# A streaming-encoder layer on one core: the second latent up projection and the chunk heads' output projection taken in turn, and latent units that wait for half of an up projection

## The chip, the core and the metric

The kernel runs on one core of a Trainium2 chip. The metric is the device time of one execution in microseconds (us). Five engines take part, each with its own queue of instructions that it works through in order: TensorE (PE, matrix multiply; its weight loads are shown as PEld), VectorE (DVE), ScalarE (ACT), GpSimd (POOL) and SyncE (SP), which here issues all DMA transfers. Matrix products land in PSUM banks and are moved to SBUF by ACT or DVE.

## The reference, cut to what matters

The sequence has 1024 rows of 1024 columns. One layer is computed:

```python
h = modulate(rmsnorm(x, g_attn_norm), sh_a, sc_a)
proj = h @ w_in                           # split into q_lat 256, kv_lat 128, k_rope 32, ca_qkv 1536
q  = rmsnorm(q_lat) @ w_q_up              # latent up projections: 8 heads x 96
kv = rmsnorm(kv_lat) @ w_kv_up            # 8 heads x (64 + 64)
o_mla = mla_attention(rope(rmsnorm(q)), rope(rmsnorm(k)), v)   # causal by chunks of 64, 8 latent heads
o_ca  = chunk_attention(cq, ck, cv, rel_bias)                  # band of 9 chunks, 8 chunk heads
x = x + g_a * (concat([o_mla, o_ca]) @ w_out)
h = modulate(rmsnorm(x, g_mlp_norm), sh_m, sc_m)
u = causal_dwconv(h @ w_up)               # 2 x 2816 columns
x = x + g_m * ((silu(gate) * val) @ w_down)
```

The rows of `w_out` fall in two halves: 0 to 511 multiply the latent heads' output, 512 to 1023 the chunk heads' output. So half of the output projection can be done as soon as all chunk heads are done.

## The kernel before, in words

Products in full precision are made of three matmuls of a high and a low part (`gemm3`, L207; `gemm3_f`, L219, the same cut into steps). The layer runs in three parts: the entry and the attention (to about 644 us of the span), the output projection of the latent heads with the second norm (to about 700 us), and the channel MLP with the two big projections. The change touches the attention part alone.

**Units.** The attention is cut into 32 units (list `specs`, L1184): 16 chunk units (0 to 15) and 16 latent units (16 to 31). A unit is one head and one half `g` of its query rows; units alternate `g` = 0 (4 key blocks) and `g` = 1 (8 key blocks). A unit has a preparation (`prep`: transposes of q and k, the tiles `mq_ps` and `mk_ps` for latent units, and their copies into `qt` and `kt`), four `guard` steps (a score pass for the row minimum), `mrow`, then per key block `st` (scores `tc` or `tm`, exponential into `p`, a high and a low half `hl`) and `val` (the product with the values, `pv`). The high half is made by ACT or, for every second block, by POOL (L1053, L1055). While unit n runs its blocks, unit n+2 is prepared and unit n+1 is guarded.

**Fillers.** Projections are generators that are advanced between the blocks (`fillers`, L1131): the chunk heads' input projections `v0`, `qk1` to `qk3`, `v1`, the latent projection `m` (L709), the two latent up projections `up0` and `up1` (`f_up`, L833; `up0` feeds latent units 16 to 23, `up1` units 24 to 31), and `oca` (L885), the chunk heads' half of the output projection. `pace` (L1178) compares the attention cost so far with a polyline `knots` (L1174) and advances the first filler in the list until its cost is on the line; up-projection steps count 3.2 times their cost (`UP_W`). `need` (L1164) advances the fillers without regard to pace until a named one has ended; a latent unit's preparation calls it with `up0` or `up1`.

**An up projection** works on 8 row tiles t. Per tile: a product `qu` (6 matmuls of 384 columns), a product `ku` (3 matmuls of 512 columns), copies by ACT (`uqr` L794, `kraw` L807, `vm` L601), squares (L796, L811), sums by DVE; and per pair of tiles an inverse root, scalings (DVE L823, ACT L828) and the rotary part on POOL (L829, L704 to L707). The scaled rows are `qn` and `kn`, which the preparations transpose.

**The chunk heads' output projection** `oca` makes 16 products (2 column halves n, 8 row tiles t), each of 12 matmuls of 512 columns (two steps of 6). Its weights come through `wo_steps` (L844): per part of 256 columns a load `wor`, a gating by POOL (L860, times the gate row in `gabc`), a high part by ACT (L81) and a low part by POOL (L87). The first set of weights is advanced once per step in the second half of `up1` (L837 to L839), and what is left of it is taken all at once when `oca` begins (L903). Each product's left side is loaded from DRAM (`cl`) and split into `ch` and `cl`, in tiles of the pool "R" that the projections use too.

The instructions are written in this order, but a scheduler then sets the final order on each engine: attention instructions have a higher priority (`OFF_S`, `OFF_V`), and filler instructions are held behind named earlier ones (`tied`, `trail`).

Of the kernel before, what the change touches and what calls it, by code (L numbers as in the profile page):

```python
# [46 lines left out]
SIDE = 1150  # L47
HI_ON, HL_BUFS = "pa", 3
VSCALE = 2.0 ** 14
O_EARLY = 0.2  # L50
UP_W = 3.2


C_C, C_GA, C_GM, C_B, C_GQL, C_GKL = 0, 8, 16, 24, 72, 74
# [14 lines left out]
def layer_kernel(ctx, tc, I, out):  # L69
# [517 lines left out]
            qk_norm(pt[:], f"{p}_{t}", qns[p, t // 4], t % 4)  # L587

    def v_tiles(pl, name, n):
        vs = [pl.tile([P, 4, 2, 3, 64], F16, name=f"{name}{i}") for i in range(n)]  # L590
# [164 lines left out]
    def f_up_steps(gr):  # L755
# [27 lines left out]
        for t in range(NT):  # L783
            h, j = divmod(t, 4)
            sl = slice(j * P, (j + 1) * P)
            if t % 2 == 0:
                mq[gr, t // 2] = g3([P, 2, 4, QK], F32, f"qn{gr}_{t}")
                mk[gr, t // 2] = g3([P, 2, 4, QK], F32, f"kn{gr}_{t}")
                mv[gr, t // 2] = G["vs"][4 * gr + t // 2]
# [41 lines left out]


    def f_up(gr):  # L833
        steps_in[0] = 0
        for c in f_up_steps(gr):
            yield c * UP_W
            steps_in[0] += gr  # L837
            if steps_in[0] > 8 * gr and gr:
                next(wo_next[0], None)  # L839

    gab = []
    wos = {}

    def wo_steps(k0, n):  # L844
        parts = [(k, c) for k in range(k0, k0 + 4) for c in range(2)]
        raws = []
        ws = wos[k0, n] = []

        def load(i):
            if i < len(parts):  # L850
                k, c = parts[i]
                raws.append(atile(f"wor{k}_{n}_{c}"))
                c0 = n * 512 + c * 256
                sp.dma_start(raws[i][:], I["w_out"][k * P:(k + 1) * P, c0:c0 + 256])

        def gated(i):
            if i < len(parts):
                c0 = n * 512 + parts[i][1] * 256
                with tied("p"):
                    pool.tensor_tensor(raws[i][:], raws[i][:], gab[0][:, c0:c0 + 256], op=MUL)  # L860

        load(0)
        load(1)
        yield
        gated(0)
        yield
        for i, (k, c) in enumerate(parts):
            load(i + 2)
            gated(i + 1)
            if c == 0:  # L870
                ws.append(g4([P, 2, 512], F32R, f"wo{k}_{n}"))
            cc = slice(c * 256, c * 256 + 256)
            tied_hi_lo(ws[-1][:, 0, cc], ws[-1][:, 1, cc], raws[i][:])
            yield

    def first_wo():
        while not ga_done:
            next(side[0])
        gab.append(pgtile([P, D], F32, "gabc"))
        sp.dma_start(gab[0][:], ga_d[:])  # L880
        yield from wo_steps(4, 0)

    wo_next = [first_wo()]

    def f_oca():  # L885
        cl, ch, xo = {}, {}, {}
        todo = [(n, t) for n in range(2) for t in range(NT)]

        def load(i):
            if i < len(todo):  # L890
                n, t = todo[i]
                cl[i] = rtile(f"cl{t}_{n}", (P, 4, P), F32R)
                sp.dma_start(f32(cl[i][:]), oT_d[4:8, :, t * P:(t + 1) * P].rearrange("k p t -> p k t"))

        def conv(i):
            if i < len(todo):
                n, t = todo[i]
                ch[i] = rtile(f"ch{t}_{n}", (P, 4, P), F32R)
                tied_hi_lo(ch[i][:], cl[i][:], f32(cl[i][:]))

        load(0)
        load(1)
        for _ in wo_next[0]:  # L903
            pass
        conv(0)
        yield 0
        for i, (n, t) in enumerate(todo):
            if t == 0:
                for _ in wo_next[0]:
                    pass  # L910
                ws = wos[4, n]
                wo_next[0] = wo_steps(0, 0) if n else wo_steps(4, 1)
            o = qtile(f"co{t}_{n}")
            sp.dma_start(o[:], I["x"][t * P:(t + 1) * P, n * 512:(n + 1) * 512])
            load(i + 2)
            conv(i + 1)
            pt = ps.tile([P, 512], F32, name=f"oc{t}_{n}", tag="mm", bufs=2)
            hi, lo = ch.pop(i), cl.pop(i)
            for c in gemm3_f(pt[:], [(hi[:, k], lo[:, k], ws[k][:, 0], ws[k][:, 1]) for k in range(4)]):
                yield c  # L920
                next(wo_next[0], None)
            with tied("v"):
                dve.tensor_tensor(o[:], o[:], pt[:], op=ADD)
            sp.dma_start(part_d[t][:, n * 512:(n + 1) * 512], o[:])


    NK, NQ = 4, 3
    kts = [at.tile([P, 2, 512], F16, name=f"kt{i}") for i in range(NK)]
# [180 lines left out]
    def mla_unit(n, gr, hh, g):  # L1109
        u = Unit(n, f"m{gr}{hh}", g, False, hh % 2,  # L1110
                 lambda b: (mv[gr, b // 2], 2 * (b % 2) + hh // 2),
                 oT_d[2 * gr + hh // 2][64 * (hh % 2):64 * (hh % 2) + 64], ("m", gr))

        def prep():
            with tc.high_priority(offset=OFF_S):
                pt = turned(lambda j: mq[gr, (4 * g + j) // 2][:, j % 2, hh, :], QK, f"mq{gr}{hh}_{g}")
                sq = scm[:QK, 2:3]
                act.activation(u.q[:QK, 0], pt[:QK], AF.Copy, scale=sq)
                dve.scalar_tensor_tensor(u.q[:QK, 1], pt[:QK], sq, u.q[:QK, 0], op0=MUL, op1=SUB)
                pt = turned(lambda j: mk[gr, (4 * g + j) // 2][:, j % 2, hh, :], QK, f"mk{gr}{hh}_{g}")  # L1120
# [12 lines left out]
    spent = [0.0]  # L1133
    done = set()
    side = [f_ada()]
# [5 lines left out]
    def fill_step():  # L1141
        while fillers:
            key, gen = fillers[0]
            if key == "oca" and not ca_done or key == "v1" and not p0_done:
                return None
            try:
                c = next(gen)
# [1 line left out]
                done.add(key)  # L1149
                fillers.pop(0)  # L1150
                continue
            spent[0] += c
            if key not in ("v0", "up0", "up1", "oca"):
                nside[0] += c
                while nside[0] > SIDE:
                    nside[0] -= SIDE
# [7 lines left out]
    def need(keys):  # L1164
        for k in keys:
            while k not in done:
# [486 lines left out]
```

## Time and profile before

| | |
|---|---|
| median of 3 runs | 1395.44 us (1393.77 to 1395.97) |
| the profiled execution | 1393.72 us, its span 1391.5 us |
| mean granted TensorE clock | 0.962 |
| chunk units' scores `tc` | from 87 to 406 us of the span |
| up projections' products `qu`, `ku` | from 357 to 474 us |
| latent units' scores `tm` | from 419 to 641 us |
| chunk heads' output products `oc` | from 491 to 639 us |
| latent heads' output products `op` | from 651 to 700 us |

A table of stretches has one row for each stretch of the span: its length, then for PE, PEld, DVE, ACT and POOL the busy time and in brackets the number of instructions, then the granted clock of TensorE (1.00 is full speed), the share of DMA time and GB/s. A row of the timeline has the start, the duration, engine, line, operation, output <- input, and in square brackets how long the engine sat idle before and what it waited for. A row of a tile's view has the shortest, median and longest duration in ns and the first and last start.

### The profile page before, as it was taken

To read this page: it belongs to the slowest core of one execution; us is meant where nothing else is said; L and a number is where in the kernel's file an instruction comes from. 1 tells how busy PE (TensorE), PEld (TensorE's weight loads), DVE (VectorE), ACT (ScalarE), POOL (GpSimd) and SP (SyncE) were. 2 spreads that over 40 slices of the span, in tenths; PEclk is the share of its full clock that TensorE was granted. 3 is DMA by queue.
4 is the path that set the end of the run, shared out by engine and by line. 5 is a ranking of instruction groups with operands and counts; after the bars stand their busy time and mean duration, and the time that the engine had idled before them with its cause. 6 is when DMAs were issued, how large, how long until landed. Compare 5 with 4: busy or idle time off the path is not lost.

```text
span 1391.5 us, 20573 instructions
## 1 busy us (share of the span) xinstructions
PE 1295.8 (93%) x7140; PEld 884.3 (64%) x7140; DVE 1029.7 (74%) x1512; ACT 817.3 (59%) x1584; POOL 745.1 (54%) x844
## 2 busy tenths in 40 slices
PE   8888999999878899997989989999999979999998
PEld 7877788878545466555844434444444438888887
DVE  7758887776668867674679989888888875566564
ACT  5646676566778767664786566666666533333331
POOL 5844434244453572443533876666666626666563
PEclk7999999999979899998999999999999989999999
DMA  9412333222000243225516422222211006446443
GB/s 352 135 39 79 100 100 96 79 77 62 24 23 20 59 142 96 87 95 183 214 46 234 144 98 92 91 91 92 82 71 61 31 31 219 151 144 244 163 145 106
DMA packets 85764, 153.06 MB, mean 110 GB/s; under 512 B 8854, under 2 KB 49050, under 8 KB 85660
## 3 DMA queue, kind: packets, MB, share of 16 engines
q1 hardware_dynamic: 85660, 151.75, 32.6%
q8 instruction: 56, 0.92, 0.3%
q14 instruction: 48, 0.39, 0.1%
HBM read 122.88 MB, written 28.84 MB: 109 GB/s over the span
## 4 chain that ended last, share of the span: by engine, by line
PE 68%; DVE 12%; ACT 6%; POOL 5%; issue 5%; DMA 4%; SPq 0%; POOLq 0%; ACTq 0%; DVEq 0%
PE p L1326 8%; PE p L1325 8%; PE p L1327 8%; PE dn L1567 6%; PE dn L1568 6%; PE dn L1569 6%; PE tm L1045 3%; PE tc L1045 1%; DMA aw<-w_ada 1%; PE op L211 1%; DMA x<-x 1%; PE op L213 1%; PE op L212 1%; PE oc L211 1%; PE pvm L1072 1%
## 5 line engine op out<-in xcount | busy, mean ns | idle before, releaser
L87 POOL TENSOR_TENSOR wds<-wd,wds 128x512 fp32r<-128x512 f32 x88 | 152.4, 1752 | 104.2 <-ACT wds L81 104.1
L1567 PE MATMUL dn<-wds,g 128*128 128x512 f32 x352 | 136.8, 395 | 9.1 <-ACT g L81 9.1
L81 ACT ACTIVATE wds<-wd 128x512 fp32r<-128x512 f32 x88 | 54.7, 624 | 152.4 <-PE dn L1569 152.4
L1568 PE MATMUL dn<-wds,g 128*128 128x512 f32 x352 | 136.7, 391 | 0.0
L1554 DVE TENSOR_TENSOR wd<-wd,gmbc 128x1024 f32<-128x1024 f32 x44 | 73.8, 1680 | 84.1 <-DMA wd<-w_down 84.1
L1569 PE MATMUL dn<-wds,g 128*128 128x512 f32 x352 | 135.3, 389 | 0.0
L1056 DVE TENSOR_TENSOR hlm<-pm,hlm 128x512 f16<-128x512 f32 (+1 forms) x96 | 64.6, 682 | 35.7 <-POOL hlm L83 22.4
L1406 ACT ACTIVATE u<-c,pk,wcv 128x1024 f32<-128x1024 f32 x44 | 52.2, 1232 | 51.1 <-DVE c L1446 43.9
L1567 PEld LDWEIGHTS dn<-wds,g 128*128 128x128 f32 x352 | 67.1, 191 | 23.7 <-ACT g L81 9.6
L87 DVE TENSOR_TENSOR g<-gr,g 128x512 fp32r<-128x512 f32 x44 | 71.0, 1614 | 6.7 <-ACT g L81 6.4
L1568 PEld LDWEIGHTS dn<-wds,g 128*128 128x128 f32 x352 | 66.6, 189 | 13.7
L1045 PE MATMUL tm<-qt,kt 96*128 96x512 f16 (+7 forms) x288 | 69.6, 338 | 6.0 <-ACT hlm L1053 2.4
L1569 PEld LDWEIGHTS dn<-wds,g 128*128 128x128 f32 x352 | 66.1, 188 | 13.8
L83 POOL TENSOR_SCALAR hlm<-pm 128x384 f16<-128x384 f32 (+2 forms) x48 | 25.2, 525 | 92.4 <-PE pvm L1074 44.7
L1407 DVE SCALAR_TENSOR_TENSOR u<-c,wcv,u 128x1023 f32<-128x1023 f32 x44 | 56.0, 1308 | 24.4 <-ACT u L1406 24.4
L1049 ACT ACTIVATE pm<-tm,scm 128x512 f32<-128x512 f32 (+1 forms) x96 | 55.2, 580 | 31.4 <-PE tm L1045 24.0
L1056 DVE TENSOR_TENSOR hlc<-pc,hlc 128x256 f16<-128x256 f32 (+3 forms) x96 | 52.1, 547 | 22.5 <-POOL hlc L83 11.7
L1045 PEld LDWEIGHTS <-kt 128*128 128x128 f16 (+2 forms) x480 | 45.7, 100 | 34.9 <-issue 16.9
L1049 ACT ACTIVATE pc<-tc,sca 128x512 f32<-128x512 f32 (+3 forms) x96 | 50.3, 525 | 29.9 <-DVE hlc L1056 13.4
L1002 DVE TENSOR_REDUCE mz<-sm 128x1 f16<-128x128 f32 (+3 forms) x64 | 48.2, 753 | 20.4 <-PE sm L1000 17.3
L81 ACT ACTIVATE wd<-wu 128x512 f16<-128x512 f32 x22 | 13.9, 630 | 83.6 <-DVE wu L1337 83.6
L1318 POOL TENSOR_TENSOR wa<-wu,wa 128x512 f16<-128x512 f32 x22 | 35.4, 1609 | 50.3 <-ACT wa L81 50.1
(470 smaller groups left out, 4551.0 us busy)
## 6 DMA issues: line engine op xcount, KB each, us to landing
wu<-w_up SPq DMA_DIRECT2D x44, 512.0 KB, 4.0
wd<-w_down SPq DMA_DIRECT2D x44, 512.0 KB, 3.6
aw<-w_ada SPq DMA_DIRECT2D x96, 128.0 KB, 2.2
g_d<-u SPq DMA_DIRECT2D x22, 512.0 KB, 2.6
gr<-g_d SPq DMA_DIRECT2D x44, 256.0 KB, 3.0
adaw<-w_ada_a SPq DMA_DIRECT2D x16, 512.0 KB, 6.8
x<-x SPq DMA_DIRECT2D x8, 512.0 KB, 7.5
wq_r<-w_qk SPq DMA_DIRECT2D x32, 128.0 KB, 2.4
```

Of the source, the lines that this page charges most:

```text
L81: return act.activation(o, i, AF.Copy)
L87: return (pool if eng == "p" else dve).tensor_tensor(o, i, f32(hi), op=SUB)
L1045: last = pe.matmul(s[:, c0:c1], l, m, start=(y == 0), stop=(y == len(todo) - 1))
L1049: recent["a"] = act.activation(p[:, :w], s[:, :w], AF.Exp, scale=ninv)
L1056: lo = recent["v"] = dve.tensor_tensor(hl[:, 1, :w], p[:, :w], hl[:, 0, :w], op=SUB)
L1325: pe.matmul(pt, sh, pg[:, 0], start=(k == 0), stop=False)
L1326: pe.matmul(pt, sh, pg[:, 1], start=False, stop=False)
L1327: pe.matmul(pt, sl, pg[:, 0], start=False, stop=(k == 3))
L1554: dve.tensor_tensor(raw[:], raw[:], gmbc[:], op=MUL)
L1567: pe.matmul(pts[t][n], sh, w[n][:, 0], start=(j == 0), stop=False)
L1568: pe.matmul(pts[t][n], sh, w[n][:, 1], start=False, stop=False)
L1569: pe.matmul(pts[t][n], sl, w[n][:, 0], start=False, stop=(j == NF - 1))
```

## The change

`f_mix` takes the place of `up1` and `oca` in the list of fillers. It advances the two generators in turn once the chunk heads are done and the first set of output weights has been prepared; until then it advances `up1` alone, and every call prepares a step of those weights first. An up projection marks its first half (row tiles 0 to 3) as done under a name of its own (`up0a`, `up1a`), and a latent unit with `g` = 0 waits only for that. The pace is set anew: `up1` steps count 2.0 times instead of 3.2, all of `up0` is due one chunk unit earlier (13 instead of 14 units), and half of `up1` and `oca` together is due at the sixth latent unit. The gate row and the left sides of `oca` now lie over the chunk heads' value tiles `vca`, which are free by then, and `oca` splits the next left side in its first step and loads the one after in its second. In the diff, lines that only carry new names are left out.

```diff
-O_EARLY = 0.2
-UP_W = 3.2
+MID = 0.5
+UP_W = (3.2, 2.0)
...
         for t in range(NT):
             h, j = divmod(t, 4)
             sl = slice(j * P, (j + 1) * P)
+            if t == 4:
+                done.add(f"up{gr}a")
...
     def f_up(gr):
-        steps_in[0] = 0
         for c in f_up_steps(gr):
-            yield c * UP_W
-            steps_in[0] += gr
-            if steps_in[0] > 8 * gr and gr:
-                next(wo_next[0], None)
+            yield c * UP_W[gr]
...
+    def over_v(i, name, dt=F32):
+        return at.tile([P, 768], dt, name=name, tag=f"vca{i}", bufs=1)[:, :512]
+
-    def wo_steps(k0, n):
+    def wo_steps(k0, n, each=1):
...
             tied_hi_lo(ws[-1][:, 0, cc], ws[-1][:, 1, cc], raws[i][:])
-            yield
+            if i % each == each - 1:
+                yield
 
     def first_wo():
         while not ga_done:
             next(side[0])
-        gab.append(pgtile([P, D], F32, "gabc"))
-        sp.dma_start(gab[0][:], ga_d[:])
-        yield from wo_steps(4, 0)
+        for n in range(2):
+            gab.append(over_v(n, f"gabc{n}"))
+            sp.dma_start(gab[n], ga_d[:, n * 512:(n + 1) * 512])
+        yield from wo_steps(4, 0, 2)
...
-                cl[i] = rtile(f"cl{t}_{n}", (P, 4, P), F32R)
+                cl[i] = over_v(2 + i % 2, f"cl{t}_{n}", F32R).rearrange("p (k t) -> p k t", k=4)
...
-                ch[i] = rtile(f"ch{t}_{n}", (P, 4, P), F32R)
+                ch[i] = over_v(4 + i % 2, f"ch{t}_{n}", F32R).rearrange("p (k t) -> p k t", k=4)
...
         load(0)
+        yield 0
+        conv(0)
         load(1)
-        for _ in wo_next[0]:
-            pass
-        conv(0)
         yield 0
...
-            load(i + 2)
-            conv(i + 1)
...
-            for c in gemm3_f(pt[:], [(hi[:, k], lo[:, k], ws[k][:, 0], ws[k][:, 1]) for k in range(4)]):
+            for x, c in enumerate(gemm3_f(pt[:], [(hi[:, k], lo[:, k], ws[k][:, 0], ws[k][:, 1]) for k in range(4)])):
+                if x == 0:
+                    conv(i + 1)
+                else:
+                    load(i + 2)
                 yield c
                 next(wo_next[0], None)
...
+    def f_mix():
+        gens = {"up1": f_up(1), "oca": f_oca()}
+        prepared, turn = False, 0
+        while gens:
+            if ca_done and not prepared:
+                prepared = next(wo_next[0], 1) is not None
+            turn += 1
+            if "up1" in gens and ("oca" not in gens or not prepared or turn % 2):
+                key = "up1"
+            elif prepared:
+                key = "oca"
+            else:
+                yield None
+                continue
+            c = next(gens[key], None)
+            if c is None:
+                gens.pop(key)
+                done.add(key)
+            else:
+                yield c
...
-        u.need = [f"up{gr}"]
+        u.need = [f"up{gr}" + ("" if g else "a")]
...
-               ("m", f_m()), ("up0", f_up(0)), ("up1", f_up(1)), ("oca", f_oca())]
+               ("m", f_m()), ("up0", f_up(0)), ("mix", f_mix())]
...
-    W_IN, W_M, W_UP, W_O = 21.0e3, 36.4e3, 13.0e3 * UP_W, 41.5e3
-    W_A = 5 * W_IN + W_M + W_UP
+    W_IN, W_M, W_UP, W_O = 21.0e3, 36.4e3, 13.0e3, 41.5e3
+    W_A = 5 * W_IN + W_M + W_UP * UP_W[0]
+    W_B = W_UP * UP_W[1] + W_O
     C_CA, C_M = 6.95e3, 8.05e3
-    knots = [(0.0, INIT * W_IN), (14 * C_CA, W_A), (16 * C_CA + 6 * C_M, W_A + W_UP + O_EARLY * W_O),
-             (16 * C_CA + 16 * C_M, W_A + W_UP + W_O), (1e9, 1e9)]
+    knots = [(0.0, INIT * W_IN), (13 * C_CA, W_A), (16 * C_CA + 6 * C_M, W_A + MID * W_B),
+             (16 * C_CA + 16 * C_M, W_A + W_B), (1e9, 1e9)]
```

More of the change, by code (lines that the diff above doesn't have):

```diff
@@ L589, in v_tiles @@
     def v_tiles(pl, name, n):
-        vs = [pl.tile([P, 4, 2, 3, 64], F16, name=f"{name}{i}") for i in range(n)]
+        vs = [pl.tile([P, 4, 2, 3, 64], F16, name=f"{name}{i}", tag=f"{name}{i}", bufs=1) for i in range(n)]
         for v in vs:
@@ L857, in gated @@
             if i < len(parts):
-                c0 = n * 512 + parts[i][1] * 256
+                c0 = parts[i][1] * 256
                 with tied("p"):
-                    pool.tensor_tensor(raws[i][:], raws[i][:], gab[0][:, c0:c0 + 256], op=MUL)
+                    pool.tensor_tensor(raws[i][:], raws[i][:], gab[n][:, c0:c0 + 256], op=MUL)
         load(0)
@@ L891, in load @@
                 n, t = todo[i]
-                cl[i] = rtile(f"cl{t}_{n}", (P, 4, P), F32R)
-                sp.dma_start(f32(cl[i][:]), oT_d[4:8, :, t * P:(t + 1) * P].rearrange("k p t -> p k t"))
+                cl[i] = over_v(2 + i % 2, f"cl{t}_{n}", F32R).rearrange("p (k t) -> p k t", k=4)
+                sp.dma_start(f32(cl[i]), oT_d[4:8, :, t * P:(t + 1) * P].rearrange("k p t -> p k t"))
         def conv(i):
@@ L897, in conv @@
                 n, t = todo[i]
-                ch[i] = rtile(f"ch{t}_{n}", (P, 4, P), F32R)
-                tied_hi_lo(ch[i][:], cl[i][:], f32(cl[i][:]))
+                ch[i] = over_v(4 + i % 2, f"ch{t}_{n}", F32R).rearrange("p (k t) -> p k t", k=4)
+                tied_hi_lo(ch[i], cl[i], f32(cl[i]))
         load(0)
+        yield 0
+        conv(0)
         load(1)
-        for _ in wo_next[0]:
-            pass
-        conv(0)
         yield 0
@@ L1143, in fill_step @@
             key, gen = fillers[0]
-            if key == "oca" and not ca_done or key == "v1" and not p0_done:
+            if key == "v1" and not p0_done:
                 return None
@@ L1151, in fill_step @@
                 continue
+            if c is None:
+                return None
             spent[0] += c
-            if key not in ("v0", "up0", "up1", "oca"):
+            if key not in ("v0", "up0", "mix"):
                 nside[0] += c
```

## The prediction

> **What bounds the kernel now.** I read the page first (shares and the clock by slices), then a table of stretches cut at the first exponentials of the attention units, then the timeline of PE where the table shows a loss, then the chain of waits for what ends that loss.
>
> ```profile
> span 1391.5 us, 20573 instructions
> PE 1295.8 (93%) x7140; PEld 884.3 (64%) x7140; DVE 1029.7 (74%) x1512; ACT 817.3 (59%) x1584; POOL 745.1 (54%) x844
> ...
> PEclk7999999999979899998999999999999989999999
> ```
>
> PE is busy almost throughout, so what an edit of order can win is PE time that is idle or run at a low clock. The table shows where that is. Its rows: chunk units 0 to 11; 12 and 13 and the start of 14; a stretch with no attention block at all; unit 15; latent units 16 to 18; 19; 20; 21; 25 and 26; 30 and 31.
>
> ```profile
> 98.80:338.80 240.00, 226.94 (x1732) 194.79 (x1730) 181.79 (x420) 157.09 (x383) 91.78 (x163) 0.99 0.28 82
> 338.80:370.80 32.00, 27.52 (x193) 19.65 (x191) 22.38 (x53) 27.19 (x64) 15.89 (x36) 1.00 0.16 45
> 370.80:396.20 25.40, 16.61 (x70) 12.75 (x70) 15.89 (x43) 20.02 (x64) 13.27 (x31) 0.79 0.08 20
> 396.20:421.60 25.40, 21.96 (x109) 14.29 (x107) 16.58 (x41) 17.95 (x46) 11.64 (x20) 0.74 0.07 23
> 421.60:459.70 38.10, 32.73 (x196) 20.21 (x195) 30.50 (x58) 29.29 (x76) 14.95 (x31) 0.91 0.09 25
> 459.70:476.00 16.30, 15.48 (x97) 9.56 (x96) 14.73 (x28) 16.15 (x41) 11.40 (x19) 1.00 0.19 56
> 476.00:486.40 10.40, 6.83 (x41) 4.11 (x40) 8.52 (x18) 7.09 (x18) 5.92 (x9) 0.74 0.28 77
> 486.40:512.50 26.10, 24.89 (x134) 16.04 (x133) 18.03 (x24) 16.20 (x36) 23.35 (x32) 0.97 0.42 128
> ...
> 563.40:576.40 13.00, 10.12 (x61) 6.21 (x60) 7.67 (x12) 6.08 (x13) 3.49 (x5) 0.87 0.24 75
> ...
> 619.80:643.70 23.90, 19.90 (x101) 10.64 (x99) 11.09 (x19) 13.94 (x25) 4.10 (x7) 0.86 0.18 55
> ```
>
> I call lost: length less PE busy times clock. It gives 15.3 us in the first row (of 240), then 4.5, 12.3 (25.4 - 16.61 x 0.79), 9.2, 8.3, 0.8, 5.4, 2.0, and in the last two rows 4.2 and 6.8. Some 53 us are lost in the rows behind 338.8 us, 21.5 of them from 370.8 to 421.6. There ACT is busy 27.19 of 32 us just before and 20.02 of 25.4 in it, while PE has 16.61.
>
> ```profile
> 372.48 0.22 PE L1074 MATMUL pvc<-hlc,vca 128*128 128x128 f16 x1
> ...
> 376.24 0.45 PE L935 MATMUL mq_ps<-ident,qn 128*96 128x128 f32 x1 [3.54 <-POOL qn L707]
> ...
> 385.12 0.60 PE L211 MATMUL ku<-wk,latT 128*128 128x512 f32 x1 [2.37 <-ACT uqr L794]
> ...
> 393.33 0.50 PE L211 MATMUL ku<-wk,latT 128*128 128x512 f32 x1 [1.89 <-DVE vm L602]
> ...
> 396.23 0.63 PE L1045 MATMUL tc<-qt,kt 65*128 65x512 f16 x1
> ```
>
> These rows of PE show the bare stretch: between the last value product of unit 14 and the first band block of unit 15 stand only the tail of the first up projection (`ku` of tile 3 to `ku` of tile 7, nine products) and the preparations that wait for it. PE waits on POOL's rotary part, on ACT's copies and on DVE: each tile is a chain through three engines with two PSUM banks under it. The idle gaps bring the clock down:
>
> ```profile
> 375.00:380.00 5.00, 3.76 (x12) 3.35 (x13) 3.15 (x8) 3.61 (x11) 1.75 (x6) 0.51 0.12 26
> ...
> 385.00:390.00 5.00, 4.88 (x18) 4.12 (x19) 2.71 (x11) 3.17 (x11) 1.40 (x5) 0.66 0.00 0
> ```
>
> The second place is unit 20, where PE waits for the first weights of the chunk heads' output projection. In the chain of waits (start, duration, what):
>
> ```profile
> 470.10 0.73 POOL wor L860
> ...
> 471.99 2.09 DMA wor<-w_out
> 474.21 0.97 POOL wor L860
> ...
> 476.08 2.45 DMA wor<-w_out
> 478.67 1.63 POOL wor L860
> ...
> 481.00 2.13 DMA wor<-w_out
> ...
> 491.65 0.69 POOL wo L87
> 492.33 1.25 POOL cl L87
> ```
>
> Gate, low part, next load, one part after the other, up to the first left side `cl` at 492.3.
>
> **The change part by part.** Durations are from the profiled execution (1393.72 us, 1.7 us under the median of 1395.44); the sum is a difference and is set against the median.
>
> *1. Half of an up projection is enough for a `g` = 0 unit, and `up0` is due a unit earlier.* The second half is now needed by unit 17, prepared in unit 15, instead of by unit 16, prepared in unit 14. In the built order the bare stretch holds four up products (`ku` 5, `qu` 6, `ku` 6, `qu` 7) instead of nine. From 372.7 to 396.2 that is 23.5 / 9 = 2.6 us each, so five of them, 13 us, leave it. They cost something elsewhere, and there ACT counts:
>
> ```profile
> L828 ACT ACTIVATE kn<-kraw,ur 128x64 f32<-128x64 f32 x32 | 8.1, 337 | 1.9 <-DVE ur L145 1.9
> L796 ACT ACTIVATE usq<-uqr 128x384 f32<-128x384 f32 x9 | 4.7, 519 | 0.0
> L794 ACT ACTIVATE uqr<-qu 128x384 f32<-128x384 f32 x8 | 3.9, 486 | 1.0 <-issue 1.0
> L811 ACT ACTIVATE kraw<-kraw 128x256 f32<-128x256 f32 x8 | 3.3, 418 | 0.0
> L807 ACT ACTIVATE kraw<-ku 128x256 f32<-128x256 f32 x8 | 3.0, 377 | 1.3 <-POOL qn L707 0.9 <-issue 0.4
> L601 ACT ACTIVATE vm<-ku 128x256 f16<-128x256 f32 x8 | 3.0, 376 | 0.0
> ```
>
> Busy time over count (an up tile has four L828 here) gives 1.01 + 0.52 + 0.49 + 0.41 + 0.38 + 0.38 = 3.2 us of ACT per tile, 8.0 us for two and a half tiles. They go mostly into 338.8 to 370.8 (the built order has 27 up matmuls in unit 13, before it was 6), where ACT has 32 - 27.19 = 4.8 us free. All hidden, the gain is 13 us; none of the 8.0 hidden, it is 5; with the chain of the tiles unbroken wherever it stands, 0. I take 7, near the unhidden value, since ACT's row is 85% busy. Range 0 to 13.
>
> Here a rule bears on the size. The rows of five microseconds above show half clock with a gap of 3.54 us (375 to 380: 0.51), but also after gaps of 2.37 us (385 to 390: 0.66). The Trainium skill, page "TensorE: Matmul & The Clock Gate", section "HAM oscillation — how this bites in real kernels", asks for no PE-idle gaps above about 3.4 us. By that rule only the first gap would cost clock, and a tail half as long would run at full speed (1376.2, the second rival); by the rows it keeps low-clock pieces (1385.4). The trace decides for the latter.
>
> *2. The first output weights are prepared from unit 16 on, two parts at a time.*
>
> ```profile
> L860 POOL TENSOR_TENSOR wor<-wor,gabc x32: 721/731/1629, 446.1 to 663.4; 128x256 f32<-128x256 f32 x32
> ...
> L87 POOL TENSOR_TENSOR wo<-wor,wo x32: 721/741/1191, 457.4 to 664.7; 128x256 fp32r<-128x256 f32 x32
> ```
>
> Before, the gating began at 446 us, since only the second half of `up1` advanced it. Now the built order has all eight gates and low parts on POOL before the end of unit 18, and the first products `oc` two units earlier: 17, 7 and 24 matmuls in units 19, 20 and 21 instead of 0, 0 and 48. So the stall of unit 20 goes, and unit 21, which is PE's own bound (24.89 of 26.1 us), is halved of its filler. The lost time there is 5.4 + 2.0 = 7.4 us; I take 4.5 of it, as units 19 to 21 still end on ACT or DVE often (16.15 and 14.73 of 16.3 in unit 19). Range 0 to 7.4.
>
> What it adds lies in the row 421.6 to 459.7. Eight gates and eight low parts are 8 x (0.731 + 0.741) = 11.8 us of POOL, with POOL busy 14.95 of 38.1 there. Queued behind them on POOL are every second high half `hl` of units 17 and 18 and the rotary part of `up1`; PE's value products wait for the former. A gate also waits for its load (2.09, 2.45, 2.13 us above), now once per two parts, four times. Nothing of it on PE's path costs 0; all four waits cost about 9. Since the row has 23 us of POOL free I take +1.5. Range 0 to +9.
>
> *3. Later latent units.* With pace and turn the `oc` matmuls fall more evenly: 18 instead of 6 in unit 26, 7 instead of 0 in unit 30, the units that now show 4.2 and 6.8 us lost.
>
> ```profile
> 638.69 0.39 PE L212 MATMUL oc<-wo,ch 128*128 128x512 f32 x1
> ...
> 639.15 0.39 PE L211 MATMUL oc<-wo,ch 128*128 128x512 f32 x1
> ```
>
> At 0.23 us from matmul to matmul (two apart here), 12 and 7 matmuls are 2.8 and 1.6 us of PE work put into idle time; but they are taken from units 25, 27 and 28, which lose cover. I take -1.5; range -4.4 to +2. The turn itself does little: in the built order one `oc` product stands before the last `ku` of `up1`.
>
> *4. What else moves.* The steeper first line of the pace brings some ten matmuls of the latent projection before unit 12, about 2 us at full clock, into a row in which PE is busy 226.94 of 240: +1.5, range 0 to +2. The load of the first `cl` now stands on SP right after unit 14's store and waits for it to land:
>
> ```profile
> oT_d<-ric SPq DMA_DIRECT2D x5, 128.0 KB, 2.2
> ```
>
> ```profile
> 392.49 2.94 SPq L766 DMA_DIRECT2D wqr<-w_qu  x2
> ```
>
> 2.2 us in which SP issues nothing; behind it are the three weight loads of `up1`, which went out at 392.5, 20 us after unit 14's last value product, since their tiles are not free sooner: 0, range to +2.2. Two loads of the gate row instead of one, tiles over `vca` instead of pool "R" (two left sides in flight, each with a whole unit's time to land), and the split of the next left side by one step later cost 0; the attention matmuls between two `oc` products hide them, and without that cover each product would wait for a load of some 2 us. The removed draining loop at the start of `oca` has nothing left to drain.
>
> Sum: -7 - 4.5 + 1.5 - 1.5 + 1.5 = -10.0 us. 1395.4 - 10.0 = 1385.4 us.
>
> **The rivals.**
>
> *POOL in unit 17 and 18 (slower).* Every gate that waits for its load holds POOL, and with it the high halves and `up1`'s rotary part. For it: 11.8 us of work and four waits of 2.1 to 2.45 us come into 38.1 us, and latent units 24 on need `up1` anyway. Against it: POOL's 14.95 of 38.1, and before, the same waits stood in units 19 to 21 with POOL busy 23.35 of 26.1. If the four waits (9.2 us) and two gates behind each half of them (4 x 0.731 = 2.9) reach PE, 12 us are added in place of 1.5, and the stall of unit 20 has only moved (part 2's 4.5 is lost): 1385.4 + 10.5 + 4.5 = 1400.4. It decides once the PE time lost between 421 and 476 us grows by more than 11.5 us.
>
> *A bigger gain by the clock.* If the shorter tail leaves PE without gaps that lower the clock, the low-clock part of 370.8 to 421.6 goes too: 16.61 x 0.21 + 21.96 x 0.26 = 9.2 us, giving 1376.2. For it: five products fewer in the bare stretch. Against it: half clock after gaps of 2.37 us, and such gaps stay. The Trainium skill, page "TensorE: Matmul & The Clock Gate", by the rule given above, would have it this way.
>
> *Nothing gained.* ACT and not the order bounds 338.8 to 421.6, the moved tiles cost there what they save (part 1 is 0), and what part 2 wins is lost by part 2's own additions up to its 4.5: 1395.4 - 0 - 4.5 + 4.5 + 1.5 - 1.5 = 1395.4. For it: ACT's 85% and 79%. Against it: PE waits in the bare stretch on POOL and DVE as well.
>
> **How the numbers follow.** Chances: the sum as forecast 0.52, the clock 0.16, nothing gained 0.12, POOL 0.20. The predicted time is that of the first, 1385.4. With every part at its better end it would be 1395.4 - 13 - 7.4 - 4.4 = 1370.6, at its worse end 1395.4 + 9 + 2 + 2 + 2.2 = 1410.6; ends do not come together, so the range reaches from just under the clock case to just under the POOL case, 1375 to 1399, which leaves out less than 0.2. The forecast's own range is 1379 to 1392. A change within 0.2% (1392.6 to 1398.2) is about what a measurement here cannot tell from none. Faster 0.52 + 0.16 + 0.02 of the third case = 0.70, same 0.08 of it, slower 0.20 + 0.02 = 0.22.
>
> **What would show it.** Part 1: the stretch between unit 14's last value product and unit 15's first block is 10 to 13 us long, and the clock between 370 and 420 us is above 0.85. Part 2: the first `oc` starts before 475 us, and no 10 us stretch of units 19 to 21 has PE under 80%. Part 3: the last `tm` ends 9 to 11 us earlier. The forecast is wrong if the bare stretch stays near 25 us, if PE's idle time between 421 and 476 us grows past 11 us with releasers `hlm` L83 or `wor` (POOL), or if units 12 to 14 lengthen by more than 12 us.

## The result and the profile after the change

The changed kernel takes 1400.85 us (median; 1399.95 to 1405.19), the kernel before, measured beside it, 1395.56 us: ratio 1.0045, 95% interval 1.0028 to 1.0063. It is slower by 0.45%; 1385.4 us was forecast, and the time lies above the range.

The profiled execution of the changed kernel took 1402.55 us, 1.7 us over its median; that of before 1393.72 us, 1.8 us under its own. So of the 9.3 us between the two spans some 3.5 belong to the two executions and not to the change. The page, span, PE's share and the clock by slices:

```profile
span 1400.8 us, 20547 instructions
...
PE 1294.3 (92%) x7140; PEld 882.4 (63%) x7140; DVE 1028.4 (73%) x1512; ACT 816.2 (58%) x1584; POOL 743.5 (53%) x844
...
PEclk6899999999899999999899999999999989999999
```

PE's work is the same; 1.5 us less busy, 9.3 us longer. The table of stretches, cut at the same units as the one of before (length, then busy time of PE, PEld, DVE, ACT and POOL with instructions, granted clock, DMA share, GB/s); the last row is new, from the end of the attention to the last addition of `op`:

```profile
101.60:354.40 252.80, 231.50 (x1742) 196.15 (x1740) 181.67 (x426) 160.76 (x397) 99.20 (x187) 0.98 0.28 83
354.40:382.90 28.50, 24.47 (x159) 17.07 (x157) 20.51 (x49) 22.74 (x58) 8.88 (x16) 0.90 0.04 10
382.90:404.00 21.10, 14.93 (x90) 10.88 (x89) 15.46 (x38) 18.93 (x55) 10.99 (x28) 1.00 0.18 49
404.00:430.40 26.40, 21.48 (x115) 14.18 (x114) 19.72 (x50) 20.99 (x58) 13.30 (x24) 0.87 0.14 43
430.40:467.10 36.70, 31.53 (x195) 19.74 (x195) 31.78 (x62) 33.67 (x90) 25.77 (x46) 0.95 0.15 44
467.10:485.40 18.30, 17.90 (x107) 10.58 (x105) 14.72 (x28) 15.65 (x37) 9.27 (x18) 1.00 0.09 22
485.40:493.90 8.50, 6.79 (x49) 4.75 (x47) 7.34 (x13) 5.94 (x11) 3.91 (x9) 0.95 0.30 95
493.90:513.70 19.80, 19.80 (x111) 11.72 (x110) 13.20 (x19) 12.53 (x25) 11.54 (x15) 0.94 0.31 94
...
645.60:711.90 66.30, 55.49 (x239) 44.88 (x240) 36.45 (x51) 33.75 (x61) 30.79 (x41) 0.87 0.53 194
```

The same last row in the kernel before:

```profile
645.70:701.30 55.60, 51.22 (x234) 42.10 (x234) 33.26 (x50) 33.57 (x61) 29.77 (x41) 0.94 0.64 232
```

From the start times in the two traces the span divides so (us):

| stretch | before | after | difference | in the prediction's sum |
|---|---|---|---|---|
| start to the first exponential | 98.8 | 101.6 | +2.8 | 0 |
| units 0 to 11 | 240.0 | 252.8 | +12.8 | +1.5 |
| units 12 to 14, to unit 15's first exponential | 58.1 | 49.6 | -8.5 | -7 |
| unit 15 to the end of the attention | 248.8 | 241.6 | -7.2 | +1.5 - 4.5 - 1.5 |
| output projection behind it | 55.6 | 66.3 | +10.7 | 0 |
| the rest | 690.2 | 688.9 | -1.3 | 0 |

Two rows are as forecast or better. The attention ends at 645.6 instead of 645.7 us: the early units take what the later ones give. The 10 us that remain arise in a stretch that the prediction did not look at.

There the trace shows the following. SP issues, around the end of the attention, first before, then after (start, time, queue, line, what):

```profile
648.23 0.98 SPq L1352 DMA_DIRECT2D x<-part_d  x2
649.71 0.33 SPq L854 DMA_DIRECT2D wor<-w_out  x1
650.10 2.01 SPq L1352 DMA_DIRECT2D x<-part_d  x2
...
656.43 1.59 SPq L1352 DMA_DIRECT2D x<-part_d  x2
658.89 3.15 SPq L1294 DMA_DIRECT2D wu<-w_up  x4
```

```profile
649.38 5.10 SPq L855 DMA_DIRECT2D wor<-w_out  x4
654.92 2.90 SPq L1380 DMA_DIRECT2D x<-part_d  x5
657.87 2.42 SPq L1322 DMA_DIRECT2D wu<-w_up  x4
660.38 2.92 SPq L1380 DMA_DIRECT2D x<-part_d  x3
```

Before, the loads of the residual stream (`x`, 512 KB each) stand between the last weight loads; after, all stand behind them, and three even behind 2 MB of up weights. The four weight loads take 5.10 us, since each waits for POOL to free its tile. From 650 to 655 us the DMA share is 0.34 against 1.00 before. PE then waits in front of the transposes for the normalized `x`, which in the built order (the order on each engine that the scheduler wrote into the program) now stand after 96 `op` matmuls and not after 117. The first of these transposes and the stretch from 650 us, before:

```profile
680.01 0.38 PE L1271 MATMUL ht_ps<-ident,x 128*128 128x128 f32 x2
```

```profile
650.00:655.00 5.00, 4.65 (x12) 3.71 (x13) 3.35 (x8) 1.66 (x4) 3.76 (x5) 0.50 1.00 310
```

There the transpose follows an `op` matmul without a wait. After (rows of PE, then stretches of five microseconds):

```profile
674.04 0.39 PE L213 MATMUL op<-wo,ol 128*128 128x512 f32 x1
679.25 0.69 PE L1299 MATMUL ht_ps<-ident,x 128*128 128x128 f32 x2 [4.82 <-DVE x L1404]
...
690.78 0.54 PE L1299 MATMUL ht_ps<-ident,x 128*128 128x128 f32 x2 [1.82 <-DVE x L1404]
```

```profile
650.00:655.00 5.00, 4.65 (x16) 3.71 (x16) 2.88 (x13) 1.63 (x4) 5.00 (x7) 0.66 0.34 107
...
675.00:680.00 5.00, 0.75 (x3) 0.56 (x4) 3.03 (x5) 5.00 (x8) 1.93 (x4) 0.73 1.07 392
680.00:685.00 5.00, 5.00 (x14) 3.84 (x15) 5.00 (x4) 2.91 (x6) 5.00 (x4) 0.58 0.11 43
685.00:690.00 5.00, 3.95 (x19) 2.87 (x17) 5.00 (x4) 2.38 (x5) 5.00 (x4) 1.00 0.00 0
690.00:695.00 5.00, 4.22 (x14) 3.41 (x15) 3.12 (x4) 2.70 (x6) 0.70 (x3) 0.66 0.22 86
```

By the prediction's measure (length less PE busy times clock) the stretch loses 66.3 - 55.49 x 0.87 = 18.0 us after and 55.6 - 51.22 x 0.94 = 7.5 before: 10.5 us more.

### The profile page after: what moved, and what is told of

It reads as the page before. It is cut to its first block, busy times and chain, and to the rows that moved or that the text cites. A ratio compares the mean times of both kernels' runs of the same rounds, so it can differ in the third digit from the quotient of the medians.

```text
span 1400.8 us, 20547 instructions
## 1 busy us (share of the span) xinstructions
PE 1294.3 (92%) x7140; PEld 882.4 (63%) x7140; DVE 1028.4 (73%) x1512; ACT 816.2 (58%) x1584; POOL 743.5 (53%) x844
## 4 chain that ended last, share of the span: by engine, by line
PE 64%; DVE 14%; ACT 8%; issue 5%; DMA 5%; POOL 3%; SPq 0%; POOLq 0%; DVEq 0%; ACTq 0%
PE p L1354 8%; PE p L1353 8%; PE p L1355 8%; PE dn L1595 6%; PE dn L1596 6%; PE dn L1597 6%; PE tm L1070 2%; PE tc L1070 2%; DVE adaw L504 1%; DVE mz L1027 1%; DMA wor<-w_out 1%; PE op L211 1%; PE op L212 1%; PE op L213 1%; PE pvm L1097 1%
## 5 line engine op out<-in xcount | busy, mean ns | idle before, releaser
L1081 DVE TENSOR_TENSOR hlm<-pm,hlm 128x512 f16<-128x512 f32 (+2 forms) x96 | 61.2, 645 | 30.0 <-ACT hlm L1078 14.8
L1081 DVE TENSOR_TENSOR hlc<-pc,hlc 128x512 f16<-128x512 f32 (+3 forms) x96 | 53.4, 562 | 31.9 <-ACT hlc L1078 16.8
L1074 ACT ACTIVATE pm<-tm,scm 128x512 f32<-128x512 f32 (+1 forms) x96 | 55.0, 579 | 33.6 <-PE tm L1070 26.7
L1070 PE MATMUL tc<-qt,kt 128*128 128x512 f16 (+3 forms) x192 | 55.1, 311 | 10.9 <-ACT hlc L1078 5.5
```

The lines of the kernel that those rows point to most:

```text
L1070: last = pe.matmul(s[:, c0:c1], l, m, start=(y == 0), stop=(y == len(todo) - 1))
L1074: recent["a"] = act.activation(p[:, :w], s[:, :w], AF.Exp, scale=ninv)
L1081: lo = recent["v"] = dve.tensor_tensor(hl[:, 1, :w], p[:, :w], hl[:, 0, :w], op=SUB)
```

## The experiments

Names: kernels that begin with `a_` start from the changed kernel, with `b_` from the kernel before. Each ratio is to the kernel before, timed beside it (its medians there are 1395.6 to 1397.2 us; where an expectation is in microseconds, the ratio times 1395.56 us is the fair comparison). The three stretches are those of the table above, taken from the profiled execution; "to unit 15" includes the start. These executions lie from 2.9 us below to 6.1 us above the median of their kernel, so a difference of a few microseconds between two rows of stretches can be the execution's.

| kernel | us | ratio, 95% interval | to unit 15 | unit 15 to end of attention | output projection |
|---|---|---|---|---|---|
| before | 1395.56 | 1 | 396.9 | 248.8 | 55.6 |
| changed | 1400.85 | 1.0045 (1.0028 to 1.0063) | 404.0 | 241.6 | 66.3 |
| a_gab | 1392.47 | 0.9971 (0.9957 to 0.9985) | 406.4 | 243.7 | 56.3 |
| b_gab | 1405.73 | 1.0065 (1.0049 to 1.0081) | 399.1 | 248.3 | 64.6 |
| a_xf | 1402.93 | 1.0058 (1.0036 to 1.0080) | 405.0 | 243.8 | 60.7 |
| b_half | 1396.91 | 1.0003 (0.9991 to 1.0015) | 397.1 | 248.9 | 55.6 |
| b_k13 | 1401.43 | 1.0039 (1.0022 to 1.0055) | 402.3 | 250.0 | 56.2 |
| a_k14 | 1406.32 | 1.0072 (1.0050 to 1.0094) | 400.3 | 242.5 | 69.4 |
| a_gab_k14 | 1392.44 | 0.9970 (0.9959 to 0.9981) | 398.7 | 243.7 | 56.9 |
| a_gab_k15 | 1393.33 | 0.9976 (0.9963 to 0.9989) | 396.5 | 249.0 | 56.3 |
| a_gab_n12_16 | 1394.44 | 0.9985 (0.9974 to 0.9997) | 399.1 | 250.2 | 56.5 |
| a_gab_k14_late | 1400.14 | 1.0030 (1.0016 to 1.0045) | 401.4 | 253.7 | 57.0 |
| b_early | 1397.90 | 1.0015 (1.0004 to 1.0027) | 400.7 | 249.6 | 55.2 |
| a_gab_k14_seq | 1397.39 | 1.0010 (0.9994 to 1.0026) | 401.0 | 246.3 | 56.9 |
| a_gab_k14_m6 | 1394.83 | 0.9983 (0.9971 to 0.9996) | 399.6 | 244.5 | 56.0 |
| a_gab_k14_m4 | 1395.54 | 0.9987 (0.9975 to 1.0000) | 398.1 | 247.5 | 55.9 |

**The place of the gate row.** `a_gab` undoes it in the changed kernel:

```diff
-        for n in range(2):
-            gab.append(over_v(n, f"gabc{n}"))
+        gabt = pgtile([P, D], F32, "gabc")
+        for n in range(2):
+            gab.append(gabt[:, n * 512:(n + 1) * 512])
             sp.dma_start(gab[n], ga_d[:, n * 512:(n + 1) * 512])
```

> The changed kernel with one thing undone: the gate row of the output weights is one tile of the page pool again, as before the change, and no longer lies over two of the chunk value tiles. Theory 'gate row': behind the attention the tiles of the stream's loads take the memory of those value tiles, so they wait for the last gate of the last output weights; the planner therefore puts these loads behind the weight loads and the transposes ahead of most of the output projection, and that is the 9.4 us between the last unit's end and the last output product. Then the stretch from the last unit's end to the last op product goes from 66 us to 56 us and the time to about 1391.5 us (ratio to the kernel before 0.997). Rival 'chunk pace': what makes the kernel slower is the later end of units 12 to 14, and the tail only shows a wait that would be there anyway: then about 1400 us.

`b_gab` makes it alone in the kernel before (`over_v`, two loads, `gab[n]`, and a tag for the value tiles):

```diff
-        gab.append(pgtile([P, D], F32, "gabc"))
-        sp.dma_start(gab[0][:], ga_d[:])
+        for n in range(2):
+            gab.append(over_v(n, f"gabc{n}"))
+            sp.dma_start(gab[n], ga_d[:, n * 512:(n + 1) * 512])
```

> The kernel before with one thing added: the gate row lies over two of the chunk value tiles, as in the changed kernel; nothing else moves. Theory 'gate row': attention as before, and the output projection behind it 9 us longer: about 1404.5 us (ratio 1.0065). Rival 'chunk pace': no change, 1395.5 us.

Both came as the theory had them: 0.9971 and 56.3 us of output projection, 1.0065 and 64.6 us. The changed kernel takes 1.0045 / 0.9971 = 1.0074 of the time of `a_gab`, 10 us more. SP's rows go with it, first `a_gab`, then `b_gab`, and the last fence is PE in `b_gab`:

```profile
652.52 0.91 SPq L1381 DMA_DIRECT2D x<-part_d  x2
653.87 0.33 SPq L855 DMA_DIRECT2D wor<-w_out  x1
...
660.71 1.40 SPq L1381 DMA_DIRECT2D x<-part_d  x2
663.10 2.57 SPq L1323 DMA_DIRECT2D wu<-w_up  x4
```

```profile
651.61 4.68 SPq L857 DMA_DIRECT2D wor<-w_out  x4
656.33 3.72 SPq L1356 DMA_DIRECT2D x<-part_d  x5
660.09 2.26 SPq L1298 DMA_DIRECT2D wu<-w_up  x4
662.69 3.52 SPq L1356 DMA_DIRECT2D x<-part_d  x3
```

```profile
682.56 0.69 PE L1275 MATMUL ht_ps<-ident,x 128*128 128x128 f32 x2 [5.88 <-DVE x L1380]
```

One edit takes the loads' order, PE's wait and the time with it, in both directions. In one detail the theory was wrong: at run time the loads of `x` do not wait for the last gate. In the changed kernel they are issued at 654.92 us, and POOL's last gate starts only after that:

```profile
656.86 0.74 POOL L861 TENSOR_TENSOR wor<-wor,gabc 128x256 f32<-128x256 f32 x1
```

What holds them is the queue: the order written out puts them behind four weight loads that wait for POOL. Nor is it the memory of these two tiles: none of the eight `x` tiles is allotted over them, and in the built order a gate row over two other value tiles gives the same sequence of loads. What is left is that the row lies in the attention's pool, which the tiles behind it follow; how the planner (the scheduler that writes the order out) weighs that was not taken apart.

`a_xf` keeps the gate row where the change put it and issues all loads of `x` ahead of the up weights:

```diff
     for t in range(4):
         load_o(t)
+        load_x(t)
+    for t in range(4, NT):
+        load_x(t)
+    for t in range(4):
         if t % 2:
             load_ff(t // 2)
```

> The changed kernel, gate row over the value tiles as changed, with all eight loads of the residual stream issued ahead of the four loads of up weights (2 MB) behind the attention. The loads still wait for the last gate, but the 2 MB no longer stand in front of three of them, and in the built order the output products of five tiles (120) stand ahead of the first transposes, not those of four (96). Theory 'order': it is the order of products and transposes and the 2 MB that lose the time, so most of the 9.4 us comes back, 1392 to 1395 us. Rival 'late loads': the loads behind the last gate are late in any order, and little comes back: 1398 to 1401 us.

1.0058, with an interval that overlaps the changed kernel's: nothing came back. The output projection is 60.7 us instead of 66.3, but the rest is 695.6 instead of 688.9. In the other fifteen executions of the table it is 688.9 to 690.8. The up weights are now issued 14.8 us behind the end of the attention and not 12.3, and ACT reads the first of them (`wj`, from `wu`) 26.7 us behind it and not 20.9. That this is what the rest loses is argued from these times, not tried. While SP stands at the last weight loads the DMA engines have little to do in either kernel (a share of 0.34 above, 0.44 from 655 to 660 us in `a_xf`), and bringing `x` forward behind them only moved the loss.

**The half up projection.** `b_half` is part 1 of the prediction alone:

```diff
+            if t == 4:
+                done.add(f"up{gr}a")
...
-        u.need = [f"up{gr}"]
+        u.need = [f"up{gr}" + ("" if g else "a")]
```

> The kernel before with part 1 of the prediction's sum alone: a latent unit of the first half waits for the first half of its up projection; pace, weights and turn as before. The prediction: the stretch without attention work between unit 14 and unit 15 gets shorter and the time falls by 7 us (0 to 13), 1388.5 us. Rival 'nothing gained, ACT-bound': the products only move to units 12 to 14, 1395.5 us. The order of loads behind the attention stays as before, so that the tail should show 56 us.

1.0003. Unit 15 begins at 397.1 us, before at 396.9. The built order of PE is the same with and without this edit, in the kernel before and in the changed one alike: the pace has drawn the whole first up projection before any unit asks for it, so the wait never binds.

**The pace.** `b_k13` changes one number of the kernel before, `a_k14` puts it back in the changed one, and `a_gab_k14` puts it back where the gate row is back too:

```diff
-    knots = [(0.0, INIT * W_IN), (14 * C_CA, W_A),
+    knots = [(0.0, INIT * W_IN), (13 * C_CA, W_A),
```

> The kernel before with the pace alone: the first line of the filler's pace ends at 13 chunk units instead of 14. The prediction priced this at +1.5 us (0 to 2), 1397 us. Rival 'chunk pace': the filler that is drawn earlier leaves the later chunk units bare, and the end of unit 12 and 14 comes up to 20 us later of which 10 are lost: 1405 us.

> The changed kernel with the pace alone undone (14 chunk units); the gate row stays over the value tiles. If the pace costs here what it costs in the kernel before (0.39%): 1395.5 us. Rival 'paid in advance': with the early weights the latent units take back what units 12 to 14 lose, as the two kernels with the gate row in the page pool say (0.9971 and 0.9970): 1400.5 us, as the changed kernel. In both cases the tail stays at about 66 us.

> The changed kernel with the gate row back in the page pool and the first line of the pace back at 14 chunk units; the rest of the change (half-wait, early preparation of weights, the turn) stays. Theory 'separate effects': the gate row costs 0.65 to 0.75% and the pace 0.39%, each by itself, so this kernel comes to 0.9971 / 1.0039 = 0.9932 of the kernel before, 1386.7 us, and unit 12 starts at 339 us as before, not at 354. Rival 'paid in advance': the steeper pace only pays early for the shorter stretch in front of unit 15; with 14 that stretch is long again and the time stays at 1392 us.

Alone the pace costs 0.39%, 5.4 us, between the two expectations. Rows of `b_k13` for units 0 to 11, 12 and 13, and 14:

```profile
101.40:353.00 251.60, 234.11 (x1742) 198.63 (x1740) 182.92 (x426) 160.98 (x397) 99.09 (x187) 0.97 0.29 83
353.00:381.10 28.10, 23.97 (x157) 16.71 (x156) 20.39 (x49) 22.66 (x57) 8.70 (x16) 0.91 0.04 10
381.10:402.30 21.20, 15.04 (x90) 10.98 (x89) 15.46 (x38) 19.03 (x56) 11.07 (x28) 1.00 0.09 24
```

Their lengths are those of the changed kernel to within 1.2 us a row. So the shorter stretch in front of unit 15 is the pace's doing, and so is the 12 us that units 0 to 11 grow by. What PE waits for in units 0 to 11 (us in total, times, the longest), before and then in `b_k13`:

```profile
PE tc L1045 <- ACT hlc L1053: 1.1, 1, 1.1
PE tc L1045 <- ACT pc L1049: 0.6, 1, 0.6
```

```profile
PE tc L1045 <- ACT pc L1049: 4.1, 5, 1.8
PE tc L1045 <- ACT hlc L1053: 2.5, 2, 1.4
```

The scores `tc` wait for ACT's exponentials for 6.6 us instead of 1.7; in the changed kernel it is 6.6 us too. More than half of it falls in units 10 and 11: from 307 to 353 us these waits are 4.0 us in `b_k13`, and before there are none from 304 to 339 us. That is about half of what these units lose more (24.5 us in `b_k13`, 15.3 before, by the measure of the prediction); the rest, and what makes ACT late there, was not followed.

In the changed kernel the pace shows no cost: with the gate row back, 0.9971 at 13 and 0.9970 at 14 units; without, 1.0045 and 1.0072, whose intervals overlap. 'Separate effects' (0.9932) does not fit. 'Paid in advance' fits the two kernels with the gate row back, but `a_k14` is slower than either theory had it: 1.0072 is 1405.6 us, where 1395.5 and 1400.5 were expected. The traces do not explain it: `a_gab` reaches unit 15 7.7 us later than `a_gab_k14` and both need 243.7 us from there, but this execution of `a_gab` was 6.1 us above its median. Why the pace costs 5 us in the one kernel and none in the other stays open.

Two other lines of the pace, both with the gate row back: 15 units, and 14 up to unit 12 with a gentle line to the end of unit 16.

```diff
-(13 * C_CA, W_A)
+(15 * C_CA, W_A)
```

> The gate row in the page pool and the first line of the pace at 15 chunk units: still less filler is drawn in units 0 to 14. Theory 'chunk pace' taken further: each chunk unit less in the line lost 5.4 us from 14 to 13, so 15 could gain another 3 to 5 us over 14: 1382 to 1384 us. Rival 'bare stretch': the built order has 90 up products in unit 15 instead of 72, the stretch without attention work grows by six to nine products of 2.6 us each of which a part is lost: 1390 to 1395 us.

```diff
-(13 * C_CA, W_A)
+(12 * C_CA, INIT * W_IN + 12 / 14 * (W_A - INIT * W_IN)), (16 * C_CA, W_A)
```

> Gate row in the page pool; the pace follows the old line of 14 up to unit 12 and then runs gently to the end of unit 16. In the built order the stretch in front of unit 16 has 66 up products and not 72, unit 14 nine and not 18; the second up projection then reaches into unit 22. If the products crowded around unit 15 are what is lost there, 2 to 4 us faster than the pace of 14: 1388 to 1390. Rival 'moved on': latent units 18 to 22 carry up products and output products together and lose it again: 1392 to 1395 us.

0.9976 and 0.9985, no gain over 0.9970. With 15 units, unit 12 begins at 323.8 us, 15 earlier than before, but from there to unit 15 it takes 72.7 us instead of 58.1. The gentle line takes 55.6 us there and then 250.2 instead of 243.7. What the pace keeps out of one stretch turns up in another.

**Early weights and the turn.** All with the gate row in the page pool. `a_gab_k14_late` prepares the weights late, `b_early` does the early preparation alone, in the kernel before, and `a_gab_k14_seq` undoes the turn:

```diff
-            if ca_done and not prepared:
+            if "up1a" in done and not prepared:
```

> As the one with the gate row in the page pool and the pace of 14, and besides the first output weights are prepared only from the second half of the second up projection on, about as before the change. The prediction's part 2 (early weights -4.5, its addition +1.5): 3 us slower than with early weights, 1389.7 us if that one is 1386.7, with the first oc two units later. Rival 'turn and later units': the gain comes from the latent units 22 to 31 and not from the early weights: no difference.

```diff
-            if steps_in[0] > 8 * gr and gr:
+            if gr and ca_done:
                 next(wo_next[0], None)
...
-        yield from wo_steps(4, 0)
+        yield from wo_steps(4, 0, 2)
```

> The kernel before with the early preparation alone: while the second up projection runs and once the chunk units are over, each of its steps advances the first output weights, two parts at a time; pace, order of up projection and output projection, gate row as before. The prediction's part 2: -4.5 + 1.5, 1392.5 us. Rival 'needs the turn': in the built order unit 20 still has no output product and unit 21 has 36 of them, so the weights are ready earlier but nothing uses them, and the time stays at 1395.5 us.

```diff
-            if "up1" in gens and ("oca" not in gens or not prepared or turn % 2):
+            if "up1" in gens and ("oca" not in gens or not prepared or True):
```

> Gate row in the page pool, pace of 14, and the turn undone: the second up projection is finished before the first output product, while the weights are prepared early as in the change. If the turn matters, the first output products come in unit 20 and not in 19, unit 21 has 36 of them and not 24, and the time goes up by 3 to 6 us, 1395 to 1398. Theory of the prediction ('the turn itself does little'): 1392.5 us, as with the turn.

1.0030, 1.0015 and 1.0010 where both together give 0.9970. Early weights without the turn gain nothing, and the turn without early weights ends behind the kernel before. The first `oc` in each (times of the first and the last start in the row): both together, weights late, turn undone, weights alone.

```profile
L211 PE MATMUL oc<-wo,ch x64: 390/472/776, 471.5 to 633.4; 128*128 128x512 f32 x64
```

```profile
L211 PE MATMUL oc<-wo,ch x64: 390/404/776, 485.3 to 646.1; 128*128 128x512 f32 x64
```

```profile
L211 PE MATMUL oc<-wo,ch x64: 390/404/587, 484.6 to 638.3; 128*128 128x512 f32 x64
```

```profile
L211 PE MATMUL oc<-wo,ch x64: 390/474/776, 497.4 to 643.8; 128*128 128x512 f32 x64
```

Only the first has output products in unit 19. Two last kernels keep both and move only the share of products that the pace wants by unit 22:

```diff
-MID = 0.5
+MID = 0.6
```

(and 0.4 in the other.)

> Gate row in the page pool, pace of 14, early weights and turn, and the share of the second up and output projection that the pace wants done by unit 22 raised from 0.5 to 0.6. In the built order units 19 and 20 have 26 and 22 output products and not 6 and 18. Theory 'cover': what the change gains are output products in the units that waited for the weights (19 to 21); more of them there keep the gain or add 1 to 3 us: 1389 to 1392 us. Rival 'late units': the products are missing in units 29 to 31, which lose it again: 1393 to 1396 us.

> The same with the share lowered to 0.4. Weights are early and the turn is there, but in the built order unit 20 has no output product and unit 21 has 18. Theory 'cover': the gain is gone, 1395 to 1399 us, as in the kernel with the turn undone (1397.4). Rival 'early weights': it is the preparation out of the way of units 19 to 21 that counts, and the gain stays: 1392 us.

0.9983 and 0.9987, about half of the gain gone in both. 0.9983 is 1393.2 us: more products in units 19 and 20 did not add to the gain, and the time lies where the rival 'late units' had it. 0.9987 is 1393.7 us, between 'cover' (1395 to 1399) and 'early weights' (1392). The intervals of both overlap that of 0.9970, so these two runs decide little. That the products in units 19 and 20 are part of the gain is the likelier reading, from the three kernels above that have none in unit 19; that they are all of it is not shown.

The best kernels are the change with the gate row left in the page pool, at 13 or 14 units: 1392.5 and 1392.4 us, 0.3% faster than before.

## Why the prediction was wrong

**The step that failed: "Two loads of the gate row instead of one, tiles over `vca` instead of pool "R" ... cost 0".** The cover was sought in the attention, among the products between two `oc`, and there nothing was lost. But the sum ended with the last unit. The gate row is read until the last weights behind the attention (POOL's last gate starts at 656.86 us, the attention ends at 645.6), so the change does not touch the attention part alone, as was said above. Put into the attention's pool, the row pushes the loads of `x` behind those weight loads on SP. That costs 0.65% alone and 0.74% in the change, 9 to 10 us, about the forecast gain (at a pace of 14 units, 1.0072 / 0.9970, even 14 us, with a wide interval). It is not the whole miss: with the row back (`a_gab`, 0.9971) the change gains 4 us and not 10.

**Part 1 (-7) had its cause wrong.** The stretch came out as forecast: unit 14's last value product to unit 15's first band block,

```profile
392.50 0.22 PE L1099 MATMUL pvc<-hlc,vca 128*128 128x128 f16 x1
...
403.14 0.60 PE L1070 MATMUL tc<-qt,kt 65*128 65x512 f16 x2
```

10.4 us against 23.5 from the end of the one to the start of the other, at clock 1.00 up to 404 us and 0.87 behind it. But the half-wait had no part in it. The counts of the built order (27 up matmuls in unit 13 for 6) were right and were credited to the wrong edit.

**Part 4's pace (+1.5, 0 to 2) was mis-sized.** It measured +5.4 us alone. Only the matmuls drawn forward were priced, by their own duration. In the first row PE is busy 231.50 us, 4.6 more than before, but the lost time goes from 15.3 to 252.8 - 231.50 x 0.98 = 25.9 us. One of the signs named, units 12 to 14 longer by 12 us, looked at the wrong place: these got 8.5 us shorter, and units 0 to 11 12.8 us longer. There PE waits longer for ACT's exponentials, which a price made of matmul durations leaves out.

**Parts 2 and 3 (-4.5 + 1.5 - 1.5) were right in mechanism** and small in size: -7.2 us from unit 15 to the end. The first `oc` comes at 471.5 us, under the 475 asked for, and the lost time of units 16 to 19 fell from 8.3 + 0.8 us to 36.7 - 31.53 x 0.95 = 6.7 and 18.3 - 17.90 = 0.4. In units 20 and 21, which part 2 priced, it fell from 7.4 us to 8.5 - 6.79 x 0.95 = 2.0 and 19.8 - 19.80 x 0.94 = 1.2, by 4.2 for the 4.5 forecast. So the POOL rival fell: its time, 1400.4 us, is within half a microsecond of the measured one by coincidence. "The turn itself does little" was wrong: without it the gain is gone. "The last `tm` ends 9 to 11 us earlier" did not come, since the chunk units had used it up.

**The other rivals.** "Nothing gained" holds for the attention as a whole, 645.6 for 645.7 us, but what part 2 won was taken by the start and units 0 to 11, not by ACT in units 12 to 15 or by part 2's own additions. "A bigger gain by the clock" came in part: the low clock in units 12 to 15 now costs 24.47 x 0.10 + 21.48 x 0.13 = 5.2 us, where it was 9.2. As for the rule named with it, the row 690 to 695 us shows 0.66 after a gap of 1.82 us; the figure of about 3.4 us in the Trainium skill, "TensorE: Matmul & The Clock Gate", section "HAM oscillation — how this bites in real kernels", would leave such a gap without effect. The trace decides against it again.

One label in the prediction's table is off: 563.4 to 576.4 us is unit 26 alone (unit 25 begins at 548.0), as its part 3 has it; no sum changes.

## What to carry to other kernels

A tile that is moved must be followed to its last reader, past the stage in which it was moved: what opens behind that pool, and in which order the loads then stand on a queue, belongs to the sum. A wait that is relaxed is worth something only if it binds; the same counts in the built order with and without it say so ahead of any run. And filler drawn earlier is not won: see what covers the units it was taken from.

## What the hardware showed besides

From 660 to 680 us in the changed kernel the DMA share stands above 1.0 in every row of five microseconds, at 407, 416, 368 and 392 GB/s: the DMA engines had next to nothing left with which to make up the 5 us in which they were a third busy. And single executions of one kernel on one chip spread widely: `a_gab`'s twelve ran from 1387.37 to 1398.56 us, 0.8%, so that here one profile per kernel places a loss but does not size three thousandths.
